# In-projection of a hybrid streaming encoder: token tiles loaded feature-major from a second host layout, row statistics by TensorE

## The chip, the cores and the metric

One core of one Trainium2 chip runs the whole program. A core has five engines with instruction queues of their own: TensorE (PE, matmuls; its weight loads are shown as PEld), VectorE (DVE), ScalarE (ACT), GpSimd (POOL) and SyncE (SP, which here only issues DMAs). The metric is the device time of one execution in microseconds, as the median of several runs.

## The reference, cut to what matters

One inference step of a one-layer encoder: a mixer (three groups of heads: GLA, HGRN2, mLSTM) and a convolutional feed-forward block, on 1,024 prompt tokens of one new stream and 32 tokens of one running stream, model width 1,024. The change concerns only the first lines, from x to the in-projection's products:

```python
def rms_norm(x, g):
    xf = x.astype(jnp.float32)
    y = xf * lax.rsqrt(jnp.mean(xf * xf, axis=-1, keepdims=True) + EPS)
    return (y * g.astype(jnp.float32)).astype(x.dtype)
...
    proj = xn @ w_in
    (gq, gk, gv, gg, gr, hq, hf, hi, hg, mq, mk, mv, mi, mf, mo) = jnp.split(proj, pts, axis=-1)
...
        h, st_new = mixer(rms_norm(x, g_mix_pre[l]), st, lb_all[l], w_in[l], gla_w_gate[l],
```

So each token's row of 1,024 features is divided by its root mean square, multiplied by a gain per feature, and projected to 3,738 columns. Everything is float32.

## The kernel before

Tokens are worked in units of 128 (units 0 to 7 are the prompt, unit 8 the 32 tokens of the running stream) and in three groups: units 0 to 2, 3 to 5, and 6, 7 and 8. For each group the function `inproj` (L369) computes the whole in-projection. Feature-major operands are needed: TensorE contracts over the partitions, so the normalized x must lie with features on the partitions, eight tiles of 128 features.

To get float32 accuracy from TensorE's faster fp32r format, each operand is split in a high part (a cast to fp32r) and a low part (the rest), and each product is three matmuls, `mm3` (L100 to L103): high x high, high x low, low x high. The normalized x of a group is kept as `xh` and `xl` (L286, one buffer each), a weight tile as `wh` and `wl` (`weights`, L337): the raw tile is loaded by SP, cast by ScalarE or DVE (L107, L109), and the rest is made by POOL or DVE (L110). In group 0 the low parts are stored to DRAM and in the later groups they are loaded again (L347).

The norm is made token-major. `scale_x` (L293) takes a unit's x tile (128 tokens x 1,024 features), sums the squares on ScalarE (L306 for unit 0 in two halves, L316 for the others), gets rstd on POOL by a power (L307 and L308, or `rstd_of`, L219) and multiplies by rstd and by the row of gains `gx`, broadcast to all partitions, on DVE (L310, L319). `norm_group` (L323) then transposes each unit with eight TensorE transposes through two PSUM tiles (L330), casts to `xh` on ScalarE (L333) and makes `xl` on DVE (L334).

The order within a group's `inproj`: `vg(0)`, the first block of token-major products (gla's values, and 26 columns for gates that go to `tgs`, L460), unit by unit right behind that unit's norm; then thirteen feature-major tiles (`feat`, L377, 24 matmuls of up to 384 tokens each into one of the three PSUM buffers called big) with the gates, convolutions and cumulative decays on DVE, ScalarE and POOL behind each; then token-major blocks 1 to 7 (`vg`, L447), of which 1 to 3 store values (L431) and 4 to 7 pass a tanh gate (L437 to L444). Weights of each block come by two DMAs of 512 KB. The last group does blocks 1 to 7 feature-major with transposes behind (L468).

The mixer of each unit (L746), a long chain of small matmuls with DVE and ScalarE work, is a side generator: the mixers of group g are merged into the in-projection of group g+1 (L1722, L1744). Beyond that, the order of instructions on each engine is found by a list scheduler at build time: it plays the program through with estimated durations and, whenever an engine is free, takes the ready instruction that stands earliest in the program, where `high_priority` moves an instruction ahead and `issue_after` ties it behind another. Tiles with the same tag share buffers, so a new tile waits for the last reader of the one before. The tags that matter: `x` (three buffers), `qe`, `k`, `b`, `q`, `gt`, `cat` (the mixer's), `th` (one buffer, the feature stage's), PSUM `big` (three) and PSUM `o` (two, the mixer's).

The x of the next group is asked for after block 2 (L722) and normalized after block 5 (L725); the scheduler issues the loads as soon as a buffer is free.

## Time and profile before

| what | before |
|---|---|
| median of 3 runs | 1356.37 us (1355.37 to 1362.55) |
| profiled execution, first to last instruction | 1355.3 us |
| TensorE matmul busy | 1310.8 us, 97% |
| TensorE weight loads busy | 1196.7 us, 88% |
| VectorE busy | 1025.2 us, 76% |
| ScalarE busy | 709.8 us, 52% |
| GpSimd busy | 317.6 us, 23% |
| mean granted TensorE clock | 0.983 |

The in-projections with the mixers beside them take roughly the first 600 us, the feed-forward block the rest. Rows of the profile read so: in a timeline, start, duration (of a run of like instructions, from the first's start to the last's end), engine, line, operation, output tile <- input tiles, shapes, count, and in brackets the idle time of the engine before it with what ended it. In a table by stage, the stretch, its length, and the busy time (instruction count) of each engine, then the granted clock, the share of time that the DMA engines were busy, and GB/s. A group's row ends with busy us, mean ns of one, and the idle time before it. Matmuls are pipelined, so a matmul's duration is longer than the distance to the next one's start.

### The profile page before, as it was taken

The page shows a single profiled execution, that of the slowest core. Times are in us where ns is not written, and L with a number is a line of the kernel's source. Part 1 is how long each engine was busy: PE and PEld are TensorE (multiplying, and loading weights), DVE is VectorE, ACT ScalarE, POOL GpSimd, SP SyncE. Part 2 cuts the span into 40 slices and gives each one's busy share as a digit, 9 for nine tenths or more (in the row PEclk, how much of TensorE's full clock was granted, in tenths as well). Part 3 has the DMA queues.
Part 4 walks back from the last instruction along what each step waited for, and adds up shares of the span by engine and source line. Part 5 has one row for each costly group of instructions (what it writes and reads, how often), then busy time and mean ns, then how long its engine had stood idle before and what let it go on. Part 6 is the DMA issues. An engine that isn't in the chain of part 4 may idle for free.

```text
span 1355.3 us, 29229 instructions
## 1 busy us (share of the span) xinstructions
PE 1310.8 (97%) x11472; PEld 1196.7 (88%) x11472; DVE 1025.2 (76%) x1921; ACT 709.8 (52%) x1362; POOL 317.6 (23%) x530
## 2 busy tenths in 40 slices
PE   6999999999999999999999999999999999999997
PEld 5999889998888887767899999999999996678885
DVE  5795649768598678876998888888888876499566
ACT  5555556555574555435654554545554545454552
POOL 4532303135032254213211212111111110010005
PEclk9999999999998989989999999999999999999998
DMA  9799778886879963454315457536455239645435
GB/s 342 241 358 363 265 244 258 278 281 211 292 230 308 336 201 125 142 182 103 128 48 188 134 133 189 134 111 180 120 147 154 82 127 397 254 161 146 141 102 124
DMA packets 126881, 269.72 MB, mean 199 GB/s; under 512 B 24167, under 2 KB 59143, under 8 KB 126663
## 3 DMA queue, kind: packets, MB, share of 16 engines
q1 hardware_dynamic: 113111, 244.78, 53.2%
q0 software_dynamic: 9120, 18.62, 7.3%
q10 hardware_dynamic: 4512, 4.46, 1.0%
q8 instruction: 90, 1.47, 0.5%
q14 instruction: 48, 0.39, 0.1%
HBM read 206.72 MB, written 86.18 MB: 216 GB/s over the span
## 4 chain that ended last, share of the span: by engine, by line
PE 63%; DVE 5%; DMA 3%; ACT 3%; issue 2%; POOL 1%; SPq 0%; DVEq 0%; POOLq 0%; ACTq 0%
PE pux L103 5%; PE pux L102 5%; PE pux L101 5%; PE puw L101 3%; PE puw L103 3%; PE puw L102 3%; PE q L101 3%; PE q L102 3%; PE q L103 3%; PE x L101 2%; PE x L102 2%; PE x L103 2%; PE puz L103 2%; PE puz L101 2%; PE puz L102 2%
## 5 line engine op out<-in xcount | busy, mean ns | idle before, releaser
L1409 DVE SCALAR_TENSOR_TENSOR y<-uu,fconv_sb,y 128x1060 f32<-128x1060 f32 x88 | 116.2, 1320 | 36.8 <-ACT y L1407 36.2
L1345 ACT COPY c<-pux 128x272 f32<-128x272 f32 (+1 forms) x132 | 49.3, 375 | 50.5 <-PE pux L103 49.8
L1407 ACT ACTIVATE y<-uu,fconv_sb 128x1060 f32<-128x1060 f32 x44 | 56.1, 1275 | 8.5 <-POOL uu L1403 7.8
L101 PE MATMUL pv<-wt_0h,xh 128*128 128x256 f32 (+1 forms) x192 | 56.3, 293 | 3.6 <-DVE xl L334 1.6
L103 PE MATMUL zp<-woh,cl 128*128 128x512 f32 (+1 forms) x144 | 57.7, 401 | 1.5 <-DVE cl L1106 1.5
L1406 POOL COPY fhalo<-uu 128x2 f32<-128x2 f32 x44 | 16.6, 376 | 180.7 <-DVE uu L1350 180.6
L101 PE MATMUL zp<-woh,ch 128*128 128x512 f32 (+1 forms) x144 | 57.8, 410 | 0.8 <-ACT ch L1105 0.8
L102 PE MATMUL zp<-wol,ch 128*128 128x512 f32 (+1 forms) x144 | 57.9, 402 | 0.0
L103 PE MATMUL pv<-wt_1h,xl 128*128 128x256 f32 (+1 forms) x192 | 55.1, 287 | 0.0
L103 PE MATMUL pv<-wt_0h,xl 128*128 128x256 f32 (+1 forms) x192 | 55.0, 286 | 0.0
L102 PE MATMUL pv<-wt_0l,xh 128*128 128x256 f32 (+1 forms) x192 | 54.8, 286 | 0.0
L101 PE MATMUL pv<-wt_1h,xh 128*128 128x256 f32 (+1 forms) x192 | 54.7, 285 | 0.0
L102 PE MATMUL pv<-wt_1l,xh 128*128 128x256 f32 (+1 forms) x192 | 54.4, 283 | 0.0
L1585 POOL TENSOR_TENSOR gss<-gss 128x1 f32<-128x1 f32 (+1 forms) x9 | 8.2, 906 | 185.0 <-ACT gjk L1578 185.0
L221 POOL TENSOR_SCALAR hrs<-hss 128x5 f32<-128x5 f32 (+3 forms) x27 | 10.1, 375 | 176.5 <-DVE hss L1015 172.6
L831 DVE COPY_PREDICATED P<-masks_sb,sc 128x352 f32<-128x352 int32 (+3 forms) x53 | 37.9, 715 | 5.9 <-PE sc L744 5.0
L101 PEld LDWEIGHTS pv<-wt_0h,xh 128*128 128x128 f32 x192 | 36.4, 190 | 5.3 <-DVE xl L334 2.1
L1403 POOL COPY uu<-uu 128x2 f32<-128x2 f32 x44 | 28.0, 637 | 38.8 <-DVE uu L1350 37.8
L101 PEld LDWEIGHTS pv<-wt_1h,xh 128*128 128x128 f32 x192 | 36.2, 189 | 0.7 <-issue 0.6
L222 POOL TENSOR_TENSOR hrs<-hrs,mhalf 128x5 f32<-128x5 f32 (+3 forms) x27 | 36.2, 1341 | 2.2
L103 PEld LDWEIGHTS pv<-wt_0h,xl 128*128 128x128 f32 x192 | 36.5, 190 | 0.2
L102 PEld LDWEIGHTS pv<-wt_0l,xh 128*128 128x128 f32 x192 | 36.5, 190 | 0.1
(1743 smaller groups left out, 5321.0 us busy)
## 6 DMA issues: line engine op xcount, KB each, us to landing
wrP<-in_w_dn SPq DMA_DIRECT2D x27, 512.0 KB, 4.4
h_d<-y SPq DMA_DIRECT2D x22, 530.0 KB, 3.7
ht<-h_d SPq DMA_DIRECT2D x22, 530.0 KB, 10.5
wt_0r<-in_w_tok SPq DMA_DIRECT2D x21, 512.0 KB, 5.7
wt_1r<-in_w_tok SPq DMA_DIRECT2D x21, 512.0 KB, 6.3
ws_d<-in_w_dn POOLq DMA_DIRECT2D x20, 512.0 KB, 8.9
wrP<-ws_d SPq DMA_DIRECT2D x20, 512.0 KB, 4.0
wt_0l<-lt_d SPq DMA_DIRECT2D x14, 512.0 KB, 4.5
```

Source lines behind the costliest of these rows:

```text
L101: pe.matmul(ps, lh[0], rh[0], start=first, stop=False, **kw)
L102: pe.matmul(ps, lh[0], rh[1], start=False, stop=False, **kw)
L103: return pe.matmul(ps, lh[1], rh[0], start=False, stop=last, **kw)
L221: pool.tensor_scalar(out, ss, 1.0 / width, eps, op0=ALU.mult, op1=ALU.add)
L222: pool.tensor_tensor(out, out, mhalf[:n, :cols], op=ALU.pow)
L831: dve.copy_predicated(dst, mk.broadcast_to([n, 11, *mk.shape[2:]]), src)
L1345: kept[name] = act.copy(t, ps)
L1403: pool.tensor_copy(u[:, GAP_P:GAP_P + 2], u[:, GAP_S - 2:GAP_S])
L1406: behind["POOL"] = pool.tensor_copy(fhalo[:, j, :], u[:, NCOL - 2:NCOL])
L1407: act.activation(y, u, AF.Identity, scale=fconv[:, j, 2:3], bias=fconv[:, j, 3:4])
L1409: dve.scalar_tensor_tensor(y, uu[i][:, s:s + NCOL], fconv[:, j, s:s + 1], y, op0=ALU.mult, op1=ALU.add)
L1585: pool.tensor_tensor(ss[:n, 0:1], ss[:n, 2:3], ss[:n, 3:4], op=ALU.add)
```

## The change

The host passes x a second time, feature-major (`xpt`: per unit 128 features-in-tile x 8 tiles x 128 tokens; `xst` the same for the 32 tokens), and the gains as a column per tile (`gmix`). The transposes, the PSUM tiles for them and the broadcast row of gains go.

Statistics: `squares` squares each unit on ScalarE in two halves and adds the eight feature tiles down to one on DVE. `scales` sums that tile over the partitions with a TensorE matmul against a column of ones, gives rstd per token (DVE, then a power on POOL), puts it on a diagonal (DVE), and spreads it to all partitions with a second matmul, ones x diagonal; ScalarE copies the result to `R`, a tile whose every row holds rstd for each token.

Group 0 multiplies x only by the gains before the split (`scale_x`), and scales its products: the feature-major ones by `R` on DVE in PSUM, the token-major ones by rstd as a scalar per partition, on ScalarE in the copies of blocks 0 to 3, on DVE in PSUM for blocks 4 to 7. Groups 1 and 2 scale x before the split, in eight DVE instructions a unit, by gain and `R`. The next group's loads are asked for after block 1, its squares after blocks 2 to 4, its statistics after 3 to 5, their spread after 4 to 6, its scaling after 5 and 6.

```diff
@@ -145,31 +145,31 @@
     def xsrc(t0, n):
         return a["xp"][t0:t0 + n, :] if t0 < SEQ else a["xs"][t0 - SEQ:t0 - SEQ + n, :]
 
-    x_in = {}
-
-    def load_x(u):
+    xt_in = {}
+
+    def load_xt(u):
         n = 128 if u < 8 else DEC
-        x = p1.tile([128, 1024], F32, tag="x", name=f"x{u}", bufs=3)
-        for c in (slice(0, 512), slice(512, 1024)) if u == 0 else (slice(0, 1024),):
-            sp.dma_start(x[:n, c], xsrc(128 * u, n)[:, c])
+        x = p1.tile([128, 8, 128], F32, tag="x", name=f"xt{u}", bufs=3)
+        for k in (slice(0, 4), slice(4, 8)) if u == 0 else (slice(0, 8),):
+            sp.dma_start(x[:, k, :n], a["xpt"][u][:, k] if u < 8 else a["xst"][:, k])
         return x
 
-    x_in[0] = load_x(0)
     def const(name, shape, dt=F32, src=None):
         t = cp.tile(shape, dt, name=name)
         if src is not None:
             sp.dma_start(t, src)
         return t
 
-    gx = p1.tile([128, 1024], F32, name="gx")
-    act.dma_start(gx, a["grows"][3:4, :].broadcast_to([128, 1024]))
+    gmix = cp.tile([128, 12], F32, name="gmix_sb")
+    act.dma_start(gmix[:, :8], a["gmix"])
+    xt_in[0] = load_xt(0)
     wraw = {}
     for _i, _ks in enumerate(VG0):
         wraw[0, _i] = p1.tile([128, len(_ks), 282], F32, tag="wr", name=f"wt0_0_{_i}r", bufs=3)
         sp.dma_start(wraw[0, _i], a["w_tok0"][:, _ks[0]:_ks[-1] + 1])
         if not _i:
-            x_in[1] = load_x(1)
-    x_in[2] = load_x(2)
+            xt_in[1] = load_xt(1)
+    xt_in[2] = load_xt(2)
     vecs = const("vecs_sb", [128, 12], F32, a["vecs"])
     gcols = const("gcols_sb", [128, 8], F32, a["gcols"])
     masks = mx.tile([128, 6, 64], I32, name="masks_sb")
@@ -189,6 +189,8 @@
     pool.memset(ident, 0.0)
     pool.affine_select(out=ident, in_=ident, compare_op=ALU.not_equal, fill=1.0, base=0,
                        pattern=[[-1, 128]], channel_multiplier=1)
+    ones = mx.tile([128, 128], F32, name="ones")
+    pool.memset(ones, 1.0)
     mhalf = const("mhalf", [128, 16])
     pool.memset(mhalf, -0.5)
     pool.memset(halo, 0.0)
@@ -289,34 +291,61 @@
                 p1.tile([128, 8, T], F32R, tag="xl", name=f"xl{g}"))
 
     xn_of, vgi, vcopies, gate = {}, [], [], []
+    rs_of, R_of = {}, {}
+
+    def R_tile(g):
+        if g not in R_of:
+            T = GROUPS[g][1] + GROUPS[g][2]
+            R_of[g] = pf.tile([128, T], F32, tag="th", name=f"R{g}", bufs=1) if g else \
+                mx.tile([128, 384], F32, tag="sq", name="R0", bufs=1)
+        return R_of[g]
+
+    sums, spreads = {}, []
+
+    def squares(u):
+
+        n = 128 if u < 8 else DEC
+        x = xt_in[u]
+        s = sums[u] = p1.tile([128, 4, 128], F32, tag="ssq", name=f"ssq{u}", bufs=2)
+        s2 = mx.tile([128, 4, 128], F32, tag=("k", "b", "q")[u] if u < 3 else "qe", name=f"sqb{u}", bufs=1 + (u == 2))
+        act.activation(s[:, :, :n], x[:, 0:4, :n], AF.Square)
+        act.activation(s2[:, :, :n], x[:, 4:8, :n], AF.Square)
+        dve.tensor_tensor(s[:, :, :n], s[:, :, :n], s2[:, :, :n], op=ALU.add)
+        dve.tensor_tensor(s[:, 0:2, :n], s[:, 0:2, :n], s[:, 2:4, :n], op=ALU.add)
+        dve.tensor_tensor(s[:, 0, :n], s[:, 0, :n], s[:, 1, :n], op=ALU.add)
+
+    def scales(g, u, off, n):
+
+        s = sums.pop(u)
+        ps = (psb if g else psm).tile([128, 512], F32, tag="big" if g else "o", name=f"ss{u}", bufs=3 if g else 2)
+        pe.matmul(ps[:n, 0:1], s[:, 0, :n], ones[:, 0:1], start=True, stop=True)
+        rs = rs_of[u] = s[:, 2, 0:1] if g else gmix[:, 8 + u:9 + u]
+        with tc.high_priority(offset=AHEAD):
+            dve.tensor_scalar(rs[:n], ps[:n, 0:1], 1.0 / 1024, EPS, op0=ALU.mult, op1=ALU.add)
+            pool.tensor_tensor(rs[:n], rs[:n], mhalf[:n, 0:1], op=ALU.pow)
+            dve.tensor_scalar(s[:n, 1, :n], ident[:n, :n], rs[:n], None, op0=ALU.mult)
+        yield
+        pe.matmul(ps[:, 128:128 + n], ones[:n], s[:n, 1, :n], start=True, stop=True)
+        with tc.high_priority(offset=AHEAD):
+            act.copy(R_tile(g)[:, off:off + n], ps[:, 128:128 + n])
+        yield
 
     def scale_x(g):
         for (u, off, n) in units_of(g):
-            x = x_in.pop(u, None)
-            x = load_x(u) if x is None else x
             if g == 0:
-                jk = mx.tile([128, 1024], BF16, tag=("gt", "cat", "k")[u], name=f"jk{u}", bufs=1)
-            else:
-                jk = mx.tile([128, 1024], BF16, tag="qe", name=f"jk{u}", bufs=1)
-            rs = p1.tile([128, 1], F32, tag="rs", name=f"rs{u}", bufs=2)
-            if u == 0:
-                ss = p1.tile([128, 2], F32, name="ss0")
-                hs = slice(0, 512), slice(512, 1024)
-                for i, c in enumerate(hs):
-                    act.activation(jk[:, c], x[:, c], AF.Square, scale=1.0 / 32, accum_out=ss[:, i:i + 1])
-                pool.tensor_scalar(rs, ss[:, 0:1], ss[:, 1:2], EPS, op0=ALU.add, op1=ALU.add)
-                pool.tensor_tensor(rs, rs, mhalf[:, :1], op=ALU.pow)
-                for c in hs:
-                    dve.scalar_tensor_tensor(x[:, c], x[:, c], rs, gx[:, c], op0=ALU.mult, op1=ALU.mult)
+                raw, x = xt_in[u], xt_in[u]
+                if u < 2:
+                    x = mx.tile([128, 8, 128], F32, tag=("gt", "cat")[u], name=f"xg{u}t", bufs=1)
+                for k in (slice(0, 4), slice(4, 8)):
+                    dve.tensor_tensor(x[:, k], raw[:, k], gmix[:, k].unsqueeze(2).broadcast_to([128, 4, 128]), op=ALU.mult)
                 xn_of[u] = x
                 yield
                 continue
-            ss = p1.tile([128, 1], F32, tag="ss", name=f"ss{u}", bufs=2)
-            with tc.issue_after(vgi[0].ins) if vgi else ExitStack():
-                act.activation(jk[:n], x[:n], AF.Square, accum_out=ss[:n])
-            rstd_of(rs[:n], ss[:n], n, 1, 1024)
-            with tc.issue_after(vgi[1].ins) if vgi else ExitStack():
-                dve.scalar_tensor_tensor(x[:n], x[:n], rs[:n], gx[:n], op0=ALU.mult, op1=ALU.mult)
+            x = xt_in.pop(u)
+            with tc.issue_after(vgi[1].ins):
+                for k in range(8):
+                    dve.scalar_tensor_tensor(x[:, k, :n], x[:, k, :n], gmix[:, k:k + 1], R_of[g][:, off:off + n],
+                                             op0=ALU.mult, op1=ALU.mult)
             xn_of[u] = x
             yield
 
@@ -324,14 +353,11 @@
         for (u, off, n) in units_of(g):
             x = xn_of[u]
             for hf in range(2):
-                ps = psb.tile([128, 4, 128], F32, tag="big", name=f"xt{u}{hf}")
-                for k in range(4):
-                    c = 512 * hf + 128 * k
-                    pe.transpose(ps[:, k, :n], x[:n, c:c + 128], ident[:n, :n])
                 s = slice(4 * hf, 4 * hf + 4), slice(off, off + n)
+                k = slice(4 * hf, 4 * hf + 4)
                 with tc.high_priority(offset=AHEAD):
-                    act.copy(xh[(slice(None), *s)], ps[:, :, :n])
-                    dve.tensor_tensor(xl[(slice(None), *s)], ps[:, :, :n], xh[(slice(None), *s)].bitcast(F32), op=ALU.subtract)
+                    act.copy(xh[(slice(None), *s)], x[:, k, :n])
+                    dve.tensor_tensor(xl[(slice(None), *s)], x[:, k, :n], xh[(slice(None), *s)].bitcast(F32), op=ALU.subtract)
             yield
 
     def weights(src, pool_, name, shape, tags=("wr", "wh", "wl"), bufs=(3, 4), eng=None, raw=None, heng=None,
@@ -381,6 +407,8 @@
             ps = psb.tile([128, 512], F32, tag="big", name=f"pf{g}_{t}")
             for k in range(8):
                 mm3(ps[:, :T], (wh[:, k, :], wl[:, k, :]), (xh[:, k, :], xl[:, k, :]), k == 0, k == 7)
+            if g == 0:
+                dve.tensor_tensor(ps[:, :T], ps[:, :T], R_of[0], op=ALU.mult)
             return ps
 
         def conv(j, ps):
@@ -428,10 +456,13 @@
             o = mx.tile([128, 256], F32, tag="vg", name=f"vg{u}_{blk}", bufs=3)
             t = t0 + off
             if blk < 4:
-                vcopies.append(act.copy(o[:n], ps[:n, :256]))
+                vcopies.append(act.copy(o[:n], ps[:n, :256]) if g else
+                               act.activation(o[:n], ps[:n, :256], AF.Copy, scale=rs_of[u][:n]))
                 (act if g or blk else pool).dma_start(v_d[t:t + n, 256 * blk:256 * blk + 256], o[:n])
                 return
             c0 = 256 * (blk - 4)
+            if g == 0:
+                dve.tensor_scalar(ps[:n, :256], ps[:n, :256], rs_of[u][:n], None, op0=ALU.mult)
             th = gate[0].tile([128, 256], F32, tag="gth", name=f"gth{u}_{blk}", bufs=3) if gate else \
                 mx.tile([128, 256], F32, tag="vth", name=f"vth{u}_{blk}", bufs=1)
             ia = tanh(th[:n], ps[:n, :256], 0.5)
@@ -456,8 +487,14 @@
                     for j, (x, w) in enumerate(((xh, 0), (xl, 0), (xh, 1))):
                         for k in range(8):
                             pe.matmul(ps[:n, :N], x[:, k, off:off + n], ws[k][w], start=j + k == 0, stop=j + k == 9)
+                if g == 0 and not blk:
+                    spreads.append(scales(g, u, off, n))
+                    next(spreads[-1])
                 if not blk:
-                    act.copy(tgs[:n, i, :], ps[:n, 256:])
+                    if g:
+                        act.copy(tgs[:n, i, :], ps[:n, 256:])
+                    else:
+                        act.activation(tgs[:n, i, :], ps[:n, 256:], AF.Copy, scale=rs_of[u][:n])
                 vg_store(blk, u, off, n, ps)
                 yield
 
@@ -509,6 +546,9 @@
                 next(scaled, None)
             yield
         yield from early
+        for s in spreads:
+            next(s)
+        spreads.clear()
 
         gg = fm = t1("r_fm")
         ig = t1("r_ig")
@@ -719,11 +759,22 @@
             return
         for blk in range(1, 8):
             yield from vg(blk)
-            if blk == 2 and g < 2:
+            if blk == 1 and g < 2:
                 for (u, off, n) in units_of(g + 1):
-                    x_in[u] = load_x(u)
+                    xt_in[u] = load_xt(u)
+            if blk in (2, 3, 4) and g < 2:
+                u, off, n = units_of(g + 1)[blk - 2]
+                squares(u)
+            if blk in (4, 5, 6) and g < 2:
+                next(spreads.pop(0))
+            if blk in (3, 4, 5) and g < 2:
+                spreads.append(scales(g + 1, *units_of(g + 1)[blk - 3]))
+                next(spreads[-1])
             if blk == 5 and g < 2:
-                for _ in scale_x(g + 1):
+                scaling = scale_x(g + 1)
+                next(scaling)
+            if blk == 6 and g < 2:
+                for _ in scaling:
                     pass
 
 
@@ -1741,6 +1792,8 @@
         if scaled:
             next(scaled)
             next(scaled)
+            for _u in range(3):
+                squares(_u)
         merge(inproj(g, *xs_, norm_group(g, *xs_), scaled), NIN, n_side)
         if g == 0:
             mixer_zeros()
...
+    gmix = np.asarray(i["g_mix_pre"])[0].reshape(8, 128).T
+    xpt = np.asarray(i["x_prompt"])[0].reshape(8, 128, 8, 128).transpose(0, 3, 2, 1)
+    xst = np.asarray(i["x_sample"])[0].reshape(DEC, 8, 128).transpose(2, 1, 0)
...
```

7 lines of the change are left out of this document (3 added, 4 removed).

## The prediction

> **What bounds the kernel now.** I read the page's busy shares and slices first, then the timeline of the first 30 us, then busy time by stage, then who waited for whom.
>
> ```profile
> span 1355.3 us, 29229 instructions
> PE 1310.8 (97%) x11472; PEld 1196.7 (88%) x11472; DVE 1025.2 (76%) x1921; ACT 709.8 (52%) x1362; POOL 317.6 (23%) x530
> PE   6999999999999999999999999999999999999997
> DVE  5795649768598678876998888888888876499566
> ```
>
> TensorE (PE) is busy in every slice but the first, so the time moves by PE work removed, by when PE starts, and by stretches in which another engine makes it stand. VectorE (DVE) is the only other engine that comes near 9 in the stage that is changed (third slice, 68 to 102 us). The profiled execution's span, 1355.3, is 0.1 below the lowest run (1355.37) and 1.1 below the median, 1356.4; I sum against the span and add the sum to the median. A measurement of this kernel can tell about 0.5% (6.8 us) from no change.
>
> ```profile
> 6.14 0.63 ACT L306 ACTIVATE jk<-x 128x512 bf16<-128x512 f32 x1 [3.69 <-DMA x<-in_xp]
> 8.13 0.90 ACT L107 CAST wt_0h<-wt_0r 128x846 fp32r<-128x846 f32 x1 [0.36 <-DMA wt_0r<-in_w_tok]
> 8.27 0.57 POOL L308 TENSOR_TENSOR rs<-rs,mhalf 128x1 f32<-128x1 f32 x1
> 8.87 1.41 DVE L310 SCALAR_TENSOR_TENSOR x<-x,rs,gx 128x512 f32<-128x512 f32 x2 [4.59 <-POOL rs L308]
> 9.68 1.97 PE L330 MATMUL xt<-ident,x 128*128 128x128 f32 x8 [9.68 <-DVE x L310]
> 10.83 0.58 ACT L333 CAST xh<-xt 128x512 fp32r<-128x512 f32 x1 [0.28 <-PE xt L330]
> 11.47 1.07 PE L458 MATMUL pv<-wt_0h,xh 128*128 128x282 f32 x3
> 12.34 1.02 PE L458 MATMUL pv<-wt_1h,xh 128*128 128x282 f32 x3
> 13.69 0.56 PE L458 MATMUL pv<-wt_0h,xl 128*128 128x282 f32 x3
> 20.25 1.05 ACT L107 CAST wf_8h<-wf_8r 128x1024 fp32r<-128x1024 f32 x1 [2.02 <-DMA wf_8r<-in_w_feat]
> 21.38 2.38 POOL L110 TENSOR_TENSOR wf_8l<-wf_8r,wf_8h 128x1024 fp32r<-128x1024 f32 x1 [2.34 <-ACT wf_8h L107]
> 26.28 0.34 PE L101 MATMUL pf<-xh,wf_8h 128*128 128x384 f32 x1
> ```
>
> PE's one long wait is the first: x lands, squares, rstd on POOL, scaling on DVE, transposes, cast, and only at 11.47 the first projection matmul.
>
> **Part 1, the start (-3.0).** The chain becomes: x lands (6.14), one DVE product of 512 columns (0.69, priced below), the cast (0.58): 7.4. Then the weights end last: wt_0r has landed by 8.13, its cast takes 0.90, so PE can start at about 9.1, 2.4 earlier. The row of gains is gone from the queue too:
>
> ```profile
> gx<-in_grows ACTq DMA_DIRECT2D x1, 512.0 KB, 5.6
> 6.00:8.00 2.00, 0.00 (x0) 0.00 (x0) 0.00 (x0) 1.44 (x4) 0.13 (x1) 1.00 1.04 420
> ```
>
> These 512 KB at the 420 GB/s of that window are 1.25 us, and the DMA share there is 1.04, so what follows lands up to that much earlier: a start at 7.9, 3.6 earlier. Against it: PE's first six projection matmuls took 1.07 and 1.02 a triple, and a later triple 0.56, so PE starts slow; the transposes used up 1.8 us of that time (9.68 to 11.47), and matmuls in their place are 1.7 triples more at 0.5 over, 0.8. In vg(0) of the first group 24 transposes go and six fp32 matmuls come (-1.2 net, priced next). Together -2.8 to -4.0. The cap is the first feature tile: wf_8h is cast when its DMA lands (20.25) and wf_8l is done at 23.76, 22.5 with the DMA 1.25 earlier, against 26.28 now: at most 4. Two things can eat of it: DVE has 4.2 us of square sums more (priced below) in the stretch in which it makes xl, and ScalarE's two copies out of vg(0)'s PSUM now wait for rstd: a matmul of 0.25, a small DVE step, the power on POOL (0.57), with the hops some 1.5 us; behind them on ScalarE stand the next unit's xh casts and wf_8h, for which PE waits. Twice that wait is all of the gain. I take -3.0, near the end that the rows price, ends 0 and -4.
>
> **Part 2, PE work in groups 1 and 2 (-2.2).**
>
> ```profile
> L330 PE MATMUL xt<-ident,x 128*128 128x128 f32 x64 | 10.6, 293 | 10.4 <-DVE x L310 9.7 <-ACT vth L113 0.7
> 19.28 0.49 PEld L330 LDWEIGHTS xt<-ident,x 128*128 128x128 f32 x4
> 19.73 0.19 PEld L103 LDWEIGHTS pv<-wt_1h,xl 128*128 128x128 f32 x1
> 342.70 0.32 PEld L330 LDWEIGHTS xt<-ident,x 32*128 32x128 f32 x4 [0.16 <-issue]
> 174.17 0.97 PEld L744 LDWEIGHTS sc<-cf_sb,x 128*128 128x128 f32 x8
> 175.16 0.26 PEld L744 LDWEIGHTS mi<-v,kt 128*32 128x32 f32 x12
> ```
>
> A transpose lasts 293 ns, but four of them push the next weight load from 19.28 to 19.73: 0.45 for four. Groups 1 and 2 lose ten such fours and two small ones (0.32): -5.1. The nearest row for the new fp32 matmuls is the one with 128x128 weights and 11 columns: eight records, four matmuls in two passes each, in 0.99 (174.17 to 175.16): 0.25 a matmul. The sum over features and the spread are one each a unit: six units, 2 x 0.25, about -2.2 net (+3.0, less a little for the unit of 32). Bounds: 0.12 and 0.4 a matmul give -3.7 and -0.3.
>
> The Trainium skill, "TensorE: Matmul & The Clock Gate", Part 4, gives about 275 ns for a transpose in a kernel's context, near the 293 of the row. If each held PE that long, 72 would be 19.8 us instead of the 8 that the spacing of weight loads gives; the trace bears out the duration, not that it is PE time. This reading is rival B.
>
> **Part 3, DVE.** It gets the work that the transposes gave up.
>
> ```profile
> 108.27 0.69 DVE L813 TENSOR_TENSOR kh<-b 128x512 f32<-128x512 f32 x1 [1.48 <-DMA b<-qkb_d]
> 113.77 0.42 DVE L856 TENSOR_TENSOR Ld<-x,k 128x256 f32<-128x256 f32 x1
> 114.11 0.28 DVE L861 TENSOR_TENSOR Qz<-x,q 128x128 f32<-128x128 f32 x1
> 64.43 0.55 DVE L573 SCALAR_TENSOR_TENSOR q<-th,pf 128x384 f32<-128x384 f32 x1 [1.26 <-ACT th L113]
> 118.32 0.42 DVE L440 SCALAR_TENSOR_TENSOR vth<-vth,pv 128x256 f32<-128x256 f32 x1
> L319 DVE SCALAR_TENSOR_TENSOR x<-x,rs,gx 128x1024 f32<-128x1024 f32 x7 | 9.4, 1349 | 4.3 <-POOL rs L222 4.3
> 35.00:86.00 51.00, 51.00 (x291) 49.88 (x290) 43.66 (x53) 28.39 (x45) 27.94 (x15) 1.00 0.83 274
> 86.00:101.00 15.00, 15.00 (x128) 15.00 (x128) 13.81 (x22) 8.56 (x16) 3.12 (x5) 1.00 1.05 374
> 101.00:134.00 33.00, 33.00 (x280) 33.00 (x279) 18.71 (x31) 16.81 (x30) 7.22 (x12) 1.00 1.00 360
> ```
>
> (The columns of the last three are PE, weight loads, DVE, ScalarE (ACT), POOL, clock, DMA.) Per unit the sums of squares cost 0.69 + 0.42 + 0.28 = 1.4. In group 0: six products of 512 in place of four scalings (equal), 13 products of a feature tile with R, in PSUM, at 0.55 = 7.2, and 12 gate tiles at 0.42 = 5.0. For groups 1 and 2: eight narrow scalings at 0.28 = 2.2 a unit instead of 1.35, plus the 1.4 and about 0.4 for rstd and the diagonal: some 8 us a group.
>
> The 7.2 fall into 35 to 86, where DVE has 7.3 idle, and PE, starting 3.0 earlier, asks for the weight splits of the token blocks 3.0 earlier: 10.2 wanted, 7.3 there, 2.9 short. From 101 to 134 DVE idles 14.3, so what is not wanted by PE can slip there; of the 2.9 I take half on the path, **+1.5** (ends 0 and 7.2). Each feature tile also stays in its PSUM buffer 0.55 longer and ScalarE waits for it; three buffers of over 4 us of matmuls each cover that, and without the cover it would be the 7.2 again. The gate tiles (+5.0) and the preparation for group 1 (+8) fall on the 14.3 idle. The ss tile holds one of the three big PSUM buffers in blocks 3 to 6; two buffers still give each consumer one tile of PE work (3 us). For both, and the preparation for group 2, **+0.5** (0 to 4).
>
> ScalarE is even: two squares of 0.63 replace one of 1.06 with its accumulator read. POOL loses one small step a unit and sets one constant. The loads of the next x move ahead of a block, on SP past two weight loads; they wait for buffers, not for their place. The unit of 32 tokens now comes in 1,024 pieces of 128 bytes, a group ahead of its use, at nothing; without that cover it would be part of C.
>
> **Part 4, the group boundaries (-0.7).**
>
> ```profile
> 132.01 1.05 ACT L316 ACTIVATE jk<-x 128x1024 bf16<-128x1024 f32 x1
> 135.75 1.26 ACT L838 ACTIVATE qe<-q,cf_sb 128x128 f32<-128x128 f32 x4
> PE xt L330 <- ACT vth L113: 0.7, 1, 0.7
> 139.50:142.60 3.10, 1.61 (x68) 1.17 (x66) 2.66 (x6) 0.97 (x3) 1.13 (x3) 1.00 0.94 305
> 142.60:146.00 3.40, 3.37 (x15) 3.37 (x16) 3.28 (x11) 1.97 (x6) 1.45 (x2) 0.51 0.53 207
> 154.45 0.40 PE L101 MATMUL pv<-wt_0h,xh 128*128 128x282 f32 x1
> 303.00:345.00 42.00, 38.71 (x548) 35.56 (x548) 34.05 (x87) 22.43 (x57) 23.91 (x31) 1.00 0.60 196
> ```
>
> The transposes' wait for a PSUM buffer (0.7) goes with them.
>
> Sum: -3.0 - 2.2 + 1.5 + 0.5 - 0.7 = **-3.9**, so 1352.5.
>
> **Rivals.**
>
> A, slower: DVE becomes the bound of group 0. For it: 13.81 of 15 busy at 86 to 101, where it makes the weight splits that PE reads next. Against it: the 14.3 idle behind. If its 7.3 us of idle time are waits that stay where they are, the 7.2 of feature products push the splits back, the 5.0 of gate products do the same from block 4 on, and the early start buys nothing: +12.2 - 2.2 - 0.7 = +9.3, 1365.7 (1360 to 1369). It decides as soon as more than about 6 of the 12.2 come ahead of a split that PE is waiting for. Chance 0.17.
>
> B: a transpose costs PE its whole 293 ns. 72 x 0.293 is 21, less 9 x 0.5 added; with part 1's 2.4 and +2.0 on DVE that is -17, 1339.5. The spacing of loads speaks against it. Chance 0.04.
>
> C: the early start is lost, with no harm from DVE: DMA share is 1.05 and 1.00 from 86 to 134, so PE only waits for weights that come no sooner. -2.2 - 0.7 + 2.0, about 1355.5. Chance 0.12.
>
> D, more: the boundaries heal. The squares shared the qe buffer with the first mixer, which began right behind them (132.01, then 135.75); they now end some 20 us earlier, so mixer matmuls can fill PE from 139.5 on, where it was busy 1.61 of 3.1 us and then got a clock of 0.51 for 3.4 us (1.7 us lost). With that and two thirds of the 4.8 us in which PE stood at both boundaries (1.5 + 3.3), -5 more: 1347.5 (1344.5 to 1350.5). Chance 0.25.
>
> **How the numbers follow.** The forecast has 0.42, its own range 1349 to 1356. The range 1345 to 1363 leaves out B, a fifth of D and two thirds of A: 0.2. Faster by over 0.5% (below 1349.6): most of D, B, and a fifth of the forecast: 0.34. Slower (above 1363.2): three quarters of A, 0.13. Within: 0.53.
>
> **What would show it.** The first L458-type matmul at 8 to 9.2 and the first pf matmul at 22.2 to 24 confirm part 1. No L330 records, and fp32 pairs spaced 0.12, confirm part 2. PE waits for wt_0l or wt_1l from DVE between 80 and 100, or for ACT behind a feature product, would be A. PE waits on DMA there would be C. A clock without the half-rate stretch near 140 would be D. The forecast is wrong if PE begins its second group (now 154.5) later than now, or over 6 us earlier.

## The result, and the profile after

The changed kernel takes 1371.03 us (median of 4, 1369.37 to 1372.95) beside 1355.87 us for the kernel before (median of 4): ratio 1.0106, 95% interval 1.007 to 1.0141. It is some 15 us slower, outside the range, on the side of rival A and beyond its price. The profiled execution took 1372.95 us, the slowest of the four; its span is 15.9 us longer than that of before.

The page of the changed kernel, to be read against the same lines of before:

```profile
span 1371.2 us, 29260 instructions
PE 1306.9 (95%) x11436; PEld 1191.2 (87%) x11436; DVE 1058.5 (77%) x2035; ACT 712.0 (52%) x1369; POOL 310.1 (23%) x522
PE   6989999999998998999989999999999999999997
DVE  7787839778788678876798888888888875499566
```

PE's busy time did not grow (1310.8 and 1306.9), so the loss is time in which PE stands: 44.5 us before, 64.3 now. The fall of 3.9 us itself says little: among traces with the same matmuls as the changed kernel's, PE's busy time is anywhere from 1300.1 (e13) to 1310.1 (e5). PE's row of tenths has 8s in the third slice and in three later ones where there were 9s. VectorE has 33 us more.

The start of the changed kernel, PE's rows first, then the chain that it waited for on VectorE, POOL and ScalarE:

```profile
7.47 1.07 PE L489 MATMUL pv<-wt_0h,xh 128*128 128x282 f32 x3 [7.47 <-ACT xh L359]
...
18.31 0.29 PE L103 MATMUL pv<-wt_2h,xl 128*128 128x282 f32 x1
18.44 0.28 PE L321 MATMUL ss<-ones,ssq 128*128 128x1 f32 x2
18.58 0.47 PE L328 MATMUL ss<-ssq,ones 128*128 128x128 f32 x2
23.28 0.80 PE L328 MATMUL ss<-ssq,ones 128*128 128x128 f32 x2 [4.23 <-DVE ssq L326]
...
25.87 0.69 PE L101 MATMUL pf<-xh,wf_8h 128*128 128x384 f32 x1
...
26.59 0.44 PE L101 MATMUL pv<-wt_0h,xh 128*128 128x282 f32 x1
...
36.55 0.44 PE L101 MATMUL pf<-xh,wf_6h 128*128 128x384 f32 x1 [0.29 <-ACT r_ig L561]
```
```profile
18.21 2.75 DVE L693 TENSOR_SCALAR gh<-gh 128x1024 f32<-128x1024 f32 x1
...
21.34 0.15 DVE L324 TENSOR_SCALAR gmix_sb<-ss 128x1 f32<-128x1 f32 x1
...
22.95 0.28 DVE L326 TENSOR_SCALAR ssq<-ident,gmix_sb 128x128 f32<-128x128 f32 x1
```
```profile
18.06 2.35 POOL L110 TENSOR_TENSOR wf_8l<-wf_8r,wf_8h 128x1024 fp32r<-128x1024 f32 x1 [1.41 <-ACT wf_8h L107]
20.36 0.79 POOL L461 DMA_DIRECT2D v_d<-vg  x1
21.59 0.94 POOL L325 TENSOR_TENSOR gmix_sb<-gmix_sb,mhalf 128x1 f32<-128x1 f32 x1 [0.44 <-DVE gmix_sb L324]
```
```profile
22.56 0.28 ACT L497 ACTIVATE tgs<-pv,gmix_sb 128x26 f32<-128x26 f32 x1 [1.72 <-POOL gmix_sb L325]
```

PE starts 4.0 us earlier (7.47 against 11.47), has done two units by 18.6, and then stands 4.23 us at the spread matmul of unit 1 (L328). None of the matmuls queued behind it runs in that time; in e5, where this matmul is issued later, PE stands at most 1.3 us at a time between 11 and 30.5. The sum was ready at 18.7. The chain behind it is a small VectorE step that stands until 21.34 behind the halving of `gh` (a row of gains for the last norm, which does not concern the change) and three short steps, then POOL's power, and the diagonal at 22.95. ScalarE's copy of `tgs`, which needs the power too, begins at 22.56, 4.1 us after the sum began. When PE goes on, a matmul of 282 columns takes 0.44 in place of 0.29 us: the granted clock from 20 to 27 us was 0.62 (the first row of the stretches below; 1.00 in before). That is a second price on top of the wait. (The Trainium skill, "TensorE: Matmul & The Clock Gate", Part 1, says that an idle window of about 3.4 us takes the clock to half rate. The trace agrees that half the rate follows a pause, but not on the length: here the clock is 0.50 from 21.8 on, 2.7 us after PE's last matmul, and in e6 it fell after a pause of 2.31 us.) The tile wf_6 begins at 36.55, in before at 32.27.

Then, in the rest of group 0, PE's three longest waits from 50 to 140 us (before: none), and stretches of the changed kernel (columns: PE, weight loads, VectorE, ScalarE, POOL, clock, DMA share, GB/s):

```profile
PE pf L101 <- ACT q L725: 2.6, 1, 2.6
PE pv L101 <- ACT pc L418: 2.3, 2, 1.6
PE pv L101 <- DVE vth L471: 1.7, 1, 1.7
```
```profile
20.00:27.00 7.00, 3.72 (x22) 2.92 (x23) 5.63 (x16) 3.42 (x9) 3.24 (x5) 0.62 1.03 416
...
90.00:104.00 14.00, 11.70 (x86) 11.29 (x85) 13.84 (x25) 8.47 (x14) 2.44 (x5) 1.00 0.99 335
104.00:140.00 36.00, 34.28 (x336) 33.63 (x335) 27.55 (x56) 20.48 (x42) 6.45 (x10) 1.00 0.97 344
...
139.50:142.60 3.10, 3.10 (x28) 3.10 (x28) 3.10 (x10) 2.10 (x7) 1.05 (x2) 1.00 0.73 288
142.60:146.00 3.40, 3.40 (x44) 3.19 (x43) 2.56 (x6) 3.37 (x7) 2.48 (x5) 1.00 0.37 116
```

The stretch from 90 to 104 in before:

```profile
90.00:104.00 14.00, 14.00 (x121) 14.00 (x120) 10.27 (x16) 5.99 (x12) 1.74 (x4) 1.00 1.07 377
```

VectorE is full from 90 to 104 (13.84 of 14) and PE is not. The longest wait ends at 70.30. ScalarE's copy of `q` had stood for a product of VectorE, and that product behind two instructions of 3.09 and 2.47 us:

```profile
63.45 3.09 DVE L635 TENSOR_TENSOR_SCAN r_m<-r_fm,r_m,r_ig 5x384 f32<-5x384 f32 x1
...
66.65 2.47 DVE L642 TENSOR_TENSOR r_ig<-r_ig,r_bb 5x384 f32<-5x384 f32 x1
69.15 0.57 DVE L411 TENSOR_TENSOR pf<-pf,R 128x384 f32<-128x384 f32 x1
```
```profile
69.75 0.49 ACT L725 ACTIVATE q<-pf 128x384 f32<-128x384 f32 x1 [2.66 <-DVE pf L411]
```

The half-rate stretch near 142 is gone, as rival D had it. No wait of PE names a DMA, and the time is far from rival C's. One DMA stands behind a wait, though: the tanh ahead of the third (1.7, `vth`) was queued on ScalarE behind a cast that had waited 3.39 us for the weights wt_1r.

Starts of the first matmul of a tile, from the traces of this and the following runs, show where the time goes (us; "out" is the first product matmul of the out-projection, "last" the last product matmul of the program that the trace names q<-P3w,P3h):

| | g0 wf_6 | g0 wf_13 | g1 wf_6 | g2 wf_6 | out | last |
|---|---|---|---|---|---|---|
| before | 32.3 | 81.2 | 177.7 | 354.1 | 498.5 | 1344.9 |
| after | 36.5 | 89.4 | 186.9 | 358.8 | 512.5 | 1360.8 |
| e1, only group 0 new | 37.7 | 91.3 | 184.6 | 363.8 | 508.2 | 1349.7 |
| e2, only groups 1, 2 new | 32.2 | 80.9 | 174.3 | 350.3 | 504.4 | 1346.0 |
| e3, no products in group 0 | 38.2 | 89.0 | 178.9 | 354.4 | 502.6 | 1353.0 |
| e9, no statistics in group 0 | 28.0 | 77.4 | 169.4 | 344.7 | 497.6 | 1339.9 |
| e10, start mended | 32.3 | 87.8 | 189.1 | 361.5 | 514.2 | 1360.4 |
| e12, mended start, only group 0 new | 31.2 | 82.8 | 177.8 | 360.0 | 503.8 | 1346.3 |
| e13, mended start, no products | 31.1 | 82.6 | 173.0 | 349.3 | 502.6 | 1347.5 |
| e14, no feature products | 36.0 | 86.8 | 187.0 | 357.9 | 511.6 | 1357.5 |
| e15, no gate scalings | 37.4 | 90.5 | 181.6 | 357.0 | 506.3 | 1355.5 |

The two columns in the middle do not compare like with like, because the scheduler moves work of the mixers past them. Of the mixers' and gates' small matmuls, 260 records stand ahead of g1 wf_6 in before, 280 to 282 in the changed kernel, e10 and e14, and 159 to 162 in the other rows; ahead of g2 wf_6 it is 1,452 in before, e1 and e12, and 1,327 in the other rows. Ahead of g0 wf_6, of g0 wf_13 and of "out" their number is the same in all rows (2,650 at "out"). So of the 15.9 us, 8.2 are lost by g0 wf_13, 14.0 by "out". Single executions of one program differ by up to 12 us here (before: 1350.4 to 1362.6), so a few us in one late column prove nothing; verdicts below go by medians.

### The profile page after: what moved, and what is told of

The parts are those of the page before. It is cut to its first block, busy times and chain, and to the rows that moved or that the text cites. A ratio compares the mean times of both kernels' runs of the same rounds, so it can differ in the third digit from the quotient of the medians.

```text
span 1371.2 us, 29260 instructions
## 1 busy us (share of the span) xinstructions
PE 1306.9 (95%) x11436; PEld 1191.2 (87%) x11436; DVE 1058.5 (77%) x2035; ACT 712.0 (52%) x1369; POOL 310.1 (23%) x522
## 4 chain that ended last, share of the span: by engine, by line
PE 70%; DVE 16%; DMA 5%; ACT 4%; issue 2%; POOL 1%; SPq 0%; DVEq 0%; POOLq 0%; ACTq 0%
PE pux L102 4%; PE pux L101 4%; PE pux L103 4%; PE pv L101 4%; PE pv L103 3%; PE pv L102 3%; PE puw L102 3%; PE puw L103 3%; PE puw L101 3%; PE q L101 3%; PE q L102 3%; PE q L103 3%; PE x L101 2%; PE x L102 2%; PE x L103 2%
## 5 line engine op out<-in xcount | busy, mean ns | idle before, releaser
L916 DVE TENSOR_TENSOR Qz<-x,qe 128x128 f32<-128x128 f32 (+1 forms) x106 | 32.4, 337 | 9.7 <-PE sc L795 9.6
L1454 POOL COPY uu<-uu 128x2 f32<-128x2 f32 x44 | 29.2, 664 | 38.3 <-DVE uu L1401 37.4
L101 PEld LDWEIGHTS pv<-wt_1h,xh 128*128 128x128 f32 x192 | 37.1, 193 | 0.1
```

The lines of the kernel that those rows point to most:

```text
L101: pe.matmul(ps, lh[0], rh[0], start=first, stop=False, **kw)
L916: dve.tensor_tensor(Qp[:, 2 * i, :, :n // 2].rearrange("p e (m c) -> p e m c", c=c), second(x4[:, f:f + 1], c).broadcast_to([128, 2, n // ...
L1454: pool.tensor_copy(u[:, GAP_P:GAP_P + 2], u[:, GAP_S - 2:GAP_S])
```

## The experiments

Three theories stood at the outset: the products and the rstd chain of group 0 hold PE up (1), the preparation of groups 1 and 2 does (2), or the order that the scheduler finds for the later stages does (3). After the first four runs the first was split: S, the rstd chain at the start; P, the products' time on VectorE; and 3 became O.

Medians and ratios are against the kernel before on the same chip, which had 1354.6 to 1355.4 in these. A difference from the changed kernel's 1371.03 compares two chips; by the ratios such differences come out up to 2 us otherwise (e9: 15.3 in place of 17.1).

**e1_g0new and e2_g0old: half of the change each.** e1 has group 0 new and `scale_x`, transposes and loads of groups 1 and 2 old (with the row of gains loaded late, in two halves); e2 the reverse.

```diff
-        merge(inproj(g, *xs_, norm_group(g, *xs_), scaled), NIN, n_side)
+        merge(inproj(g, *xs_, (norm_old if g else norm_new)(g, *xs_), scaled), NIN, n_side)   # e1
+        merge(inproj(g, *xs_, (norm_new if g else norm_old)(g, *xs_), scaled), NIN, n_side)   # e2
```


> Only the first token group is made the new way (feature-major tiles, statistics by TensorE, products scaled); groups 1 and 2 load token-major tiles, scale them and transpose them, as before. Theory 1 (the products and the rstd chain of group 0 make PE stand while group 0 is projected): most of the +15 us stays, 1365 to 1372 against 1355.9 before, and PE's wait for the cast of q behind a feature product (2.6 us near 67 to 70) is there again. Theory 2 (the preparation of groups 1 and 2, on VectorE and in a third big PSUM buffer, starves the mixers): near before, 1353 to 1358. Theory 3 (the scheduler orders the stages behind 345 us otherwise whatever is changed ahead of them): 1360 to 1366, with the loss behind 345 us kept at some 8 us although groups 1 and 2 are prepared the old way.

> The counterpart: group 0 token-major with transposes and scaled rows, groups 1 and 2 the new way. Theory 1: at or below before, 1351 to 1357 (the 2.2 us of transposes of groups 1 and 2 gained, nothing lost in group 0). Theory 2: 1362 to 1372, with PE's idle time between 345 and 600 us some 8 us above before. Theory 3: 1360 to 1366, the stages ahead of 345 us no later than before.


e1: 1361.85, ratio 1.0051 (1.0034 to 1.0068). e2: 1357.55, ratio 1.0016 (1.0001 to 1.003). Group 0's delay is in e1 and absent from e2, so theory 1 has the place of the larger part; but e1 is below its range, and e2 above before. e1's time would fit theory 3, but its condition does not hold: the loss stands ahead of 345 us. Groups 1 and 2 alone reach g1 wf_6 3.4 us earlier, with 101 matmuls fewer ahead of it, and "out" 5.9 later. The halves add up to 8.7 of 15: group 0 costs 6.5 where groups 1 and 2 are old and 13.5 where they are new, and why is open.

**e3_noprod and e4_ghlate: the products, and one instruction at the start.**

```diff
-            if g == 0:
-                dve.tensor_tensor(ps[:, :T], ps[:, :T], R_of[0], op=ALU.mult)
...
-            if g == 0:
-                dve.tensor_scalar(ps[:n, :256], ps[:n, :256], rs_of[u][:n], None, op0=ALU.mult)
```
```diff
-            dve.tensor_scalar(gh, gh, 0.5, None, op0=ALU.mult)
...
+            if g == 0 and j == 3:
+                with tc.issue_after(ins.ins):
+                    dve.tensor_scalar(gh, gh, 0.5, None, op0=ALU.mult)
```


> The changed kernel without the 13 products of a feature tile with R and the 12 scalings of a gate tile of group 0: it leaves out the row scaling of these products, so group 0's results are of unscaled rows. Theory 1: the 12.2 us of VectorE are the loss, and the time falls by 6 to 12 us, to 1359 to 1365, with PE's second group beginning at 154 to 158 instead of 166. Theory 2: group 0 gets some 3 us earlier and the rest stays, 1366 to 1370. Theory 3: group 0 is earlier but the time after 345 us shifts by an amount that has nothing to do with it; 1360 to 1372.

> The changed kernel with one VectorE instruction moved: the halving of the 1024 columns of gh, which took 2.75 us at 18.2 us and stood ahead of the square sum for which PE's row-sum matmul waited 4.2 us, is issued behind the fourth convolution of group 0. Theory 1: PE's wait at 18.9 us falls from 4.2 to 1 to 2 us, the first feature tile comes 2 to 3 us earlier (near 27.5 instead of 30.35) and the time falls by 2 to 4 us, 1367 to 1369. Theories 2 and 3: the first feature tile is earlier, the end within 1.5 us of 1371.


e3: 1366.59, ratio 1.0082 (1.0065 to 1.01): 4.4 back, not 6 to 12 (a time that theories 2 and 3 allow too), and wf_6 is as late as ever (38.2). The products are not the loss at the start. e4: 1370.12: nothing, wf_6 at 37.1. The next two-input VectorE instruction simply stood in place of the halving, and PE waited 3.4 us:

```profile
19.13 2.11 DVE L215 TENSOR_TENSOR lbt<-lbt 128x4 f32<-128x4 f32 x1
```
```profile
18.86 2.36 POOL L110 TENSOR_TENSOR wf_8l<-wf_8r,wf_8h 128x1024 fp32r<-128x1024 f32 x1 [0.92 <-ACT wf_8h L107]
```

Four columns took 2.11 us; both end at 21.2. That looks as if VectorE waited for POOL; the next run tries it.

**e6_wf8dve: is it POOL that holds VectorE?**

```diff
-eng=dve if g == 0 and t in (6,) else None
+eng=dve if g == 0 and t in (6, 8) else None
```


> The changed kernel with one instruction moved from POOL to VectorE: the low half of the weight tile wf_8, 2.35 us on POOL at 18.06. In the trace the VectorE halving of gh under it takes 2.75 us in place of 0.69, and in the run with the halving moved away the next VectorE instruction with two SBUF operands, 128x4, took 2.11 us instead of 0.15 and ended when POOL ended. If VectorE stands while POOL works on SBUF: no VectorE instruction from 17 to 23 us is over 1.3 us, the small step of the second unit's rstd is done by 20.5 instead of 21.5, PE's wait of 4.2 us falls to 3 us or less, and the time by 0 to 2 us, 1369 to 1371. If the 2.75 us has another cause (the tile gh itself, its DMA): it stays and VectorE is later by the 1.2 us that it now does itself.


1370.81. In its trace the same instructions, with POOL free:

```profile
18.34 1.23 DVE L110 TENSOR_TENSOR wf_8l<-wf_8r,wf_8h 128x1024 fp32r<-128x1024 f32 x1 [0.95 <-ACT wf_8h L107]
19.48 0.17 DVE L214 RECIPROCAL lbt<-lbt 128x4 f32<-128x4 f32 x1
19.57 0.67 DVE L693 TENSOR_SCALAR gh<-gh 128x1024 f32<-128x1024 f32 x1
20.15 0.16 DVE L215 TENSOR_TENSOR lbt<-lbt 128x4 f32<-128x4 f32 x1
20.22 0.15 DVE L324 TENSOR_SCALAR gmix_sb<-ss 128x1 f32<-128x1 f32 x1
```

0.67 in place of 2.75, and 0.16 in place of 2.11: the stand is POOL's, as forecast, and PE's wait falls to 2.3 us. (The Trainium skill, "SBUF — State Buffer", section "Who interferes with whom", says that a VectorE instruction with two SBUF inputs contends with a GpSimd instruction that reads SBUF; the rows of four columns agree. The halving has one SBUF input, so this sentence does not cover it; that it stands too is what the rows show.) The time did not move. PE waits a second time, for the third unit's `xh`, so it stands 3.7 us in all in place of 4.2; the clock is 0.50 from 22 to 28 us as before, and wf_6 begins at 36.4:

```profile
21.41 0.69 PE L328 MATMUL ss<-ssq,ones 128*128 128x128 f32 x2 [2.31 <-DVE ssq L326]
23.49 0.60 PE L101 MATMUL pv<-wt_0h,xh 128*128 128x282 f32 x1 [1.39 <-ACT xh L359]
```

**e5_startq, e7_startfeat, e10_start5: mending the start.** e5 takes the spreads out of PE's way and gives unit 2's sums a buffer; e7 also puts the feature products ahead on VectorE; e10 adds to e5 one PSUM tile for the three sums, squares and sums ahead in their queues, and wf_7l and wf_8l on VectorE.

```diff
+            with tc.issue_after(lastmm[0].ins):        # last matmul of vg(0)
                 for s in spreads:
                     next(s)
...
+        s = sums[u] = mx.tile([128, 4, 128], F32, tag="q", name="ssq2", bufs=2) if u == 2 else \
...
+            ps, c0, c1 = sst[0], u, 128 + 128 * u      # e10: one tile "o" for units 0 to 2
```


> The changed kernel with the start untied: group 0's spread matmuls (ones x diagonal of rstd) are issued behind the last matmul of the first token block instead of between its units, and the third unit's square sums get a buffer of their own, so that its scaling does not wait for the first unit's spread. Theory S (the loss of group 0 is made at the start: PE's in-order queue stands 4.2 us at a spread matmul whose diagonal VectorE makes late, then runs at a granted clock of 0.62): no PE wait over 1 us between 11 and 30 us, the feature tile wf_6 begins near 29 to 31 instead of 36.5, and 5 to 7 of the 15 us come back, 1364 to 1367. Theory P (VectorE's 25 products are the loss): wf_6 earlier, but blocks 1 to 7 catch up the old delay, 1369 to 1371. Theory O (the order of instructions in the stages behind 345 us decides): the start is earlier and the end lies anywhere from 1360 to 1372.

> The untied start, and the 13 feature products ahead of VectorE's other work in its order. Theory S with products: in addition to the untied start, PE's wait for the cast of q behind a product that is queued on VectorE (2.6 us near 68) falls below 1 us; 1361 to 1365. Theory P: 1364 to 1369, since the products take the same time of VectorE and only move. Theory O: within 5 us of the run with the untied start alone, in either direction, by what the stages behind 345 us make of it.

> The changed kernel with the start untied further than in the first attempt, in which PE had done its matmuls up to wf_8 by 30.5 and then stood for the gate rows of the third unit, whose rstd step on POOL was queued behind a weight split of 2.5 us: the three sums share one PSUM tile, so that the third unit's sum does not wait for the first unit's spread to be copied out, the sums go ahead in their queues, and the low halves of wf_7 and wf_8 are made by VectorE instead of POOL. Theory S: wf_6 begins at 30 to 32.5 instead of 36.5, and the 4 to 6 us are kept up to the end of group 0; the end 1363 to 1368. If the loss of the start has another cause, wf_6 stays at 35 or later.


e5: 1372.82; e7: 1371.54: nothing, against theory S as I had it, and in e7 PE still waits 2.3 us for the copy of `q`. In e5 PE did run through, up to wf_8's 24 matmuls, by 30.5, and then stood for the gate rows of unit 2 (rows of PE, then POOL):

```profile
32.49 0.40 PE L562 MATMUL tg<-ident,tgs 128*16 128x128 f32 x6 [2.00 <-ACT tgs L499]
```
```profile
28.88 2.54 POOL L110 TENSOR_TENSOR wf_7l<-wf_7r,wf_7h 128x1024 fp32r<-128x1024 f32 x1 [3.78 <-ACT wf_7h L107]
31.38 0.74 POOL L326 TENSOR_TENSOR gmix_sb<-gmix_sb,mhalf 128x1 f32<-128x1 f32 x1
```

rstd of unit 2 scales `tgs`, so the transposes L562 and the gates that precede wf_6 wait for it, and its power is queued behind another weight split. e10 takes that away too: wf_6 at 32.3, as expected. But little arrives at the end: 1368.45, ratio 1.009 (1.0063 to 1.0116), just above the range, and the 2.6 us below the changed kernel are not clear of the noise. At wf_6 e10 is level with before, at wf_1 5.2 us behind it, by waits for ScalarE copies that stand behind products on VectorE:

```profile
PE pf L101 <- ACT q L736: 2.6, 1, 2.6
PE pf L101 <- ACT fr L716: 2.2, 1, 2.2
```

**e9_nostats: no statistics in group 0 at all.** `squares`, `scales` and every scaling by them are taken out for g == 0, as its expectation says.


> The changed kernel without any row statistics in group 0: it leaves out the squares, sums, rstd, the spread R and all scaling by them for that group, so group 0's rows are scaled by the gains alone; tiles, loads and groups 1 and 2 are as in the change. Theory S (the rstd chain through ScalarE, VectorE, PE, VectorE, POOL and ScalarE is what PE stands for at the start, and its products for the rest of group 0): the feature tile wf_6 begins at 28 to 30 (before 32.3, changed 36.5) and group 0 ends 10 us or more ahead of the changed kernel. If the loss were in the feature-major tiles themselves (their loads, casts or the late third unit), wf_6 stays at 33 or later. For the end: with the late stages as in the changed kernel 1358 to 1362, with them as before 1350 to 1354.


1353.89, ratio 0.9993 (0.9976 to 1.001): 17 us below the changed kernel. wf_6 begins at 28.0, 4.3 earlier than in before, so the feature-major tiles do bring the early start. Taking group 0's statistics out takes the whole loss away, so that is where it is made. The 17 us are not a pure price of the new way, since this kernel does less than before, which has statistics of its own; and no gain is left at the end: the interval holds 1.

**e13_start5np, e14_nofeat, e15_nogate: how the 17 us divide.** The edits are those of e10 and e3, together or singly.


> The changed kernel with the further untied start, and without the 13 feature products and the 12 gate scalings of group 0; it leaves out the row scaling of these products (the statistics and the spread R are still made, the value blocks still scaled). Reading C (the late rstd chain and the products cover each other: PE waits for whichever comes last, so each alone hides behind the other): 1354 to 1359, 9 to 14 us below the mended start alone. Reading D (they add up): 2.6 + 4.4 below the changed kernel, 1363 to 1365.

> The changed kernel without the 13 feature products only; it leaves out the row scaling of group 0's feature tiles. If the feature products are what costs (a tile waits on VectorE's queue behind scans of 3 us before ScalarE can copy it): PE's path from wf_6 to wf_1 is 2.5 to 3 us shorter, the end 1367 to 1369. If the gate scalings are what costs: 1370 to 1372.

> The changed kernel without the 12 gate scalings only; it leaves out the row scaling of group 0's gate tiles. If these are what costs (VectorE full from 90 to 104 us, PE waiting for the gate's product and for copies behind it): PE's path from the end of the features of group 0 to group 1's wf_6 is 3 to 6 us shorter, the end 1366 to 1369. If the feature products cost: 1370 to 1372.


e13: 1361.88 (1.0048, 1.0035 to 1.0062); e14: 1372.45; e15: 1367.57 (1.0091, 1.0076 to 1.0106). Mending the start alone gave 2.6, taking out the products 4.4, both 9.1: between the two readings, nearer to D. The 2.1 us above the sum of 7.0 are less than the noise of e10, whose interval is 7 us wide, so it is not shown that they cover each other. Without the feature products PE's path from wf_6 to wf_13 is 2.0 us shorter (50.8 against 52.8), but group 1's wf_6, with about as many matmuls ahead of it, begins when it did (187.0), and the end is no earlier. Without the gate scalings "out" comes 6.2 earlier and the median is 3.5 lower, as forecast. The rest between e13 and e9, 8.0 us, belongs to what e13 still has: squares, sums, spreads, and copies that wait for rstd. Of it, 3.1 are there at wf_6 and 5.2 at wf_13. Which of these steps holds how much was not tried.

**e8_loadearly and e11_zlow: is it the order behind group 0?** e8 is the kernel before with only the loads moved behind block 1. e11 is the changed kernel with one out-projection instruction at low priority; VectorE stands there for a POOL step, with PE's splits behind it.

```diff
-            if blk == 2 and g < 2:
+            if blk == 1 and g < 2:                                     # e8
...
+            with tc.high_priority(offset=-AHEAD):                      # e11
                 dve.scalar_tensor_tensor(z[:n], z[:n], ss[:n, 3:4], gm[:n], op0=ALU.mult, op1=ALU.mult)
```


> A control: the kernel before, in which only the loads of the next group's token tiles are queued behind block 1 instead of block 2, as the change has them; no work is added or taken away. Theories S and P: 1354 to 1357, no stage moved by over 1 us. Theory O: waits of 2 to 5 us appear or vanish in the mixers of group 2 or in the out-projection, and the median differs from before by 2 us or more, in either direction.

> The changed kernel with one instruction of the out-projection, the scaling of z by its rstd and gains on VectorE, at a lower priority: the order of work differs from the changed kernel only from the out-projection on. There VectorE stood 4.99 and 3.96 us for that rstd while splits and copies for PE were queued behind it, which it did not before. Theory O: these waits go, PE's path from the first to the last out-projection matmul is 2 to 6 us shorter, and the end is at 1365 to 1369. If the out-projection is only late because it starts late: unchanged, 1370 to 1372.


e8: 1355.9, ratio 0.9998 (0.998 to 1.0015): moving the loads costs nothing at the end. One stage did move by over 1 us: g1 wf_6 begins at 175.1 in place of 177.7, with the same matmuls ahead of it, and by "out" (500.9) that is gone. e11: 1371.47, and the row that it was to remove is still there, so it tells nothing of that wait (the first row is of the changed kernel, the second of e11):

```profile
568.39 1.29 DVE L1234 SCALAR_TENSOR_TENSOR z<-z,oss,gm 128x1024 f32<-128x1024 f32 x1 [2.62 <-POOL oss L224]
```
```profile
568.79 1.28 DVE L1235 SCALAR_TENSOR_TENSOR z<-z,oss,gm 128x1024 f32<-128x1024 f32 x1 [2.62 <-POOL oss L224]
```

From "out" to "last" PE takes 846.4 us in before, 848.3 in the changed kernel and 842.3 in e9. So the stages from "out" on account for no more than 2 us of the 15, within what executions differ by (841.5 to 850.5 over the rows of the table). For the stretch from g0 wf_13 to "out", in which 5.8 us more are lost, theory O is neither shown nor excluded.

**e12_g0best: the mended start with old groups 1 and 2.** The edits of e10 on e1.


> Group 0 in the new way with the further untied start, groups 1 and 2 in the old way (token-major, transposed): the first of these experiments with its start mended. Theory S: wf_6 at 30 to 32.5, group 0 ends some 5 us earlier than in that run, and the time is 1355 to 1358, level with before, as what the earlier start of PE gains is taken back by the feature products. Below 1352 would mean that the products cost nothing once the start is mended.


1358.01, ratio 1.0015 (0.9995 to 1.0034): the mended start is worth 3.8 us here, and the time is level with before. No version that scales all of group 0's rows was faster than before.

## Why the prediction was wrong, point by point

- **Part 1 (-3.0; measured +4.3 at wf_6): the step that failed.** The first matmul came at 7.47, a little better than the 7.9 to 9.1, but the first feature matmul at 25.87, not at 22.2 to 24. The prediction saw the chain (sum, small step, power) and priced it at 1.5 us "with the hops", in ScalarE's queue only. It took 4.1 us to ScalarE's copy, and it stands in PE's own queue too (L328, and L558 through `tgs`), where PE stood 4.23 us: VectorE's step came behind an instruction that stood 2.75 us under POOL's split, the power waited for that step, and the clock fell behind PE's pause. The warning "twice that wait is all of the gain" was the right sentence with the wrong number. e9 shows what the step would have given without it: the first feature matmul at 21.72 and wf_6 4.3 earlier, a little over the cap of 4 that was worked out. Part 1 is not the whole miss, though: with the start mended only 2.6 us came back (e10, not clear of the noise; 3.8 in e12), and 8.0 of the 17 us of group 0's statistics are not divided further.
- **Part 2 (-2.2): not shown in size.** PE's busy time fell by 3.9 over the whole program (forecast: 1.2 and 2.2), but traces of equal matmuls differ by 10. Rival B needed a fall of some 16.6 (21 less 4.5), and no trace with the changed kernel's matmuls lies more than 10.7 below before; it is not borne out.
- **Part 3 (+1.5 and +0.5): wrong in size.** The 25 products cost 4.4 us with the late start and 6.6 with the mended one (e10 to e13), a difference within the noise. Two reasons failed. "Three buffers of over 4 us of matmuls each cover that" left out what a product queues behind: 3.09 and 2.47 us of other VectorE work near 63 to 69, and PE stood 2.55 for it. "The gate tiles fall on the 14.3 idle" took idle time for cover: VectorE still idles 8.4 of 36 us from 104 to 140, yet without the gate scalings 3.5 us come back (e15), while without the feature products alone nothing does (e14). And idle time read from busy shares is a poor cover where part of the engine's time is not its own, see below.
- **Part 4 and rival D: in part right.** The half-rate stretch went. What that is worth is not shown: from g0 wf_13 to g1 wf_6 e13 takes 90.4 us against 96.5 in before, but with 101 matmuls fewer in it.
- **Groups 1 and 2 (-2.2, -0.7 and part of the +0.5): +2.2 in e2**, with an interval from 0.1 to 4.1. Theirs is the smaller part of the miss where they are changed alone, and where it arises between g0 wf_13 and "out" stays open.
- **The forecast's own sign of being wrong came:** PE began its second group at 166.4, 11.9 later than before.
- **Rival A** had the engine and the side right, and its sign came (PE waiting for ScalarE behind a feature product); its top, 1369, let the early start only vanish, not turn into a loss.

## What to carry to other kernels

A statistic that is moved behind the product does not come off the path: list every consumer of it, and follow its chain through each engine's queue that it enters, PE's included, with what is queued there at that moment. A small step on an engine that also runs 2.4 us instructions can cost such an instruction per hop, and PE paid again in clock here (half the rate after it had stood for 4.2 us, and for 3.7 in two parts in e6). Before you compare when a tile begins in two kernels, count the matmuls ahead of it: a scheduler moves work past such marks, and what looks like a gain may be work still to come.

## What the runs showed of the hardware

VectorE's busy time held time in which it stood for POOL. A repeated instruction of the changed kernel, alone and under a POOL split (the last row is POOL's):

```profile
22.61 0.42 DVE L314 TENSOR_TENSOR ssq<-ssq 128x256 f32<-128x256 f32 x1
...
33.74 2.63 DVE L314 TENSOR_TENSOR ssq<-ssq 128x256 f32<-128x256 f32 x1
...
77.85 0.54 DVE L411 TENSOR_TENSOR pf<-pf,R 128x384 f32<-128x384 f32 x1
```
```profile
33.71 2.38 POOL L110 TENSOR_TENSOR wf_3l<-wf_3r,wf_3h 128x1024 fp32r<-128x1024 f32 x1
...
77.48 2.62 POOL L110 TENSOR_TENSOR wf_12l<-wf_12r,wf_12h 128x1024 fp32r<-128x1024 f32 x1 [1.41 <-ACT wf_12h L107]
```

0.42 became 2.63 us, counted as busy, and ended 0.28 us after POOL. The product of 77.85, with one operand in PSUM, took its usual 0.54 under a POOL split. An estimate, summed over the first 140 us as what instructions under a POOL split took beyond the median of their shape: some 15 us in the changed kernel (10 instructions) and about as much in before. So before's VectorE had less work of its own than its busy share said.
